# A transformer block with 32 experts on one core: the order of the source carried to both ends of the expert loop, and the softmax moved into the first expert

## The chip, the core and the metric
The kernel runs on one core of a Trainium2 chip. The core has a matrix engine (PE in the profile, with its weight loads as PEld), a vector engine (DVE), a scalar engine (ACT), a general one (POOL) and a queue engine (SP) that here only issues DMA. Each engine has its own row of instructions and works through it in order; semaphores tie the rows together. The metric is the device time of one execution in microseconds (us). The kernel before has a median of 1613.43 us over 3 runs (1612.79 to 1615.95).

## The reference
One decoder block over 512 tokens of 1024 channels: a convolution and an attention mixer first, then a mixture of experts, each behind a norm, and a final norm. The change touches only the second half:

```python
logits = hf @ w_router + b_router
top_v, top_e = lax.top_k(logits, 4)          # of 32 experts
gates = jax.nn.softmax(top_v, axis=-1)
...                                          # tokens gathered by expert
hc = xi @ w1[e] + b1[e]                      # 1024 -> 2 x 1024
g, u = hc[:, :1024], hc[:, 1024:]
hm = (u + 1) * (min(g, 7) * sigmoid(1.702 * g))      # u clipped to +-7
y  = hm @ w2[e] + b2[e]                      # 1024 -> 1024
...                                          # y weighted by its gate, added to its token
out = rms_norm(x + gate * moe, final_g)
```

## The kernel before
**Tokens and routing.** The 512 tokens are four blocks (b = 0 to 3) of 128 rows. For each block `logits` turns the normed tokens (`h2T`) and multiplies them by the router's weights into `pl`; `choose` finds the four largest logits and writes the 0/1 mask `Mb`; `places` counts, with matmuls into `prk`, at which row of its expert a token stands, and makes `hot`, the one-hot matrix by which the tokens of expert 0 are gathered (`x_mm`, matmuls into `px`; `x_out` copies them into `XT`, the instruction xT<-px). `norm_split` cuts the normed tokens into a high and a low part (`h2H`, `h2L`). After the last block the softmax of the four chosen logits follows: `nm`, four exponentials `g4` on ACT, one reciprocal, and for each block a product and a sum that spread the gates to the table `Gd` (128 tokens x 4 blocks x 32 experts).

**Ranking.** `rank_experts` sorts the experts by their count of tokens (`ms`, `pcf`, `pcp`, `kf`, `kp`, `rank`, `pmb`, `permi`): half of them are taken with up to 128 rows, the other half ("small") with up to 64, in turn. `order_places` and `order_gates` bring the tables of places and of gates into the order of the ranks by one transposition and one matmul each (`ptp`, `posT`, `pop`; `ptg`, `gT`, `pgo`, which gives `info`). From these tables `slot_hot`, `slot_mm` and `slot_out` (`pi`, `pis`, `si`) work out, for a pair of experts at a time, the token of each row (`dstx`) and its gate (`gat`).

**Experts.** The weights come in chunks of 1 MB (128x2048) through SP's DMA queue: 8 of w1 and 4 of w2 per expert. fp32 is done by splitting: ACT writes the high part `wh`, the DVE the rest `wl`; both have four buffers, and three splits are made ahead (`split_to`). A w1 chunk then costs 12 matmuls of 128x512 for a large expert (high with high, low with high, high with low). `steps` is the list of chunks, with those of w2 of an expert between those of w1 of the next. For a small expert `h_low` copies the lower half of the sums to `b1s` and `h_join` adds it by a shift matrix; `swiglu` forms `sg_s` and `sg_u`, `turn_h` transposes into `pz` and writes `hmh`; `finish` weights `y` and scatters it to the tokens.

**The end.** `bias_rows` prepares the rows of b2 times the gates (`b2s`, the tile w in the rows), `bias_part` multiplies them into eight PSUM areas of 128x512, two for each token block: those of block 1 and those of block 3 lie in one tile called ph, those of block 0 are called py and those of block 2 pz. The result of the last expert is not scattered but split (y, w<-y, w<-y,w) and added there by a one-hot matrix `place`. `joined` adds block b's sums to the tokens and squares them on ACT; `leave` takes the root (rs_v, rsx on ACT and DVE), scales and sends the block out.

**What sets the order.** A scheduler may move instructions of one engine, unless they are marked `keep_in_program_order`. The helpers MM, TR, ACT, TT, TS, STT and COPY mark what they issue while the flag `pinned` is up. It goes up ahead of the expert loop and down at the first chunk of expert 31. Reductions, maxima, reciprocals and copies that are issued directly are never marked.

## Time and profile before
| | |
|---|---|
| median of 3 runs | 1613.43 us |
| profiled execution, its span | 1611.79 us, 1610.0 us |
| PE busy | 1488.9 us, 92% of the span |
| DVE busy | 1349.4 us, 84% |
| ACT busy | 1043.4 us, 65% |
| chain that ended last, by engine | PE 55%, DVE 5%, ACT 4%, DMA 3%, issue 2% |
| splits | 352 on ACT (wh, 1913 ns each) and 352 on the DVE (wl, 2282 ns each) |

The times are those of one profiled execution, counted from its start. The front stages (convolution, attention) end at about 461 us, the experts fill the rest. Each row of a timeline is one group of instructions of one engine: start, length, engine, line, operation, output and input tile, shapes, count, and in brackets the idle time ahead of it with what ended it. Most lines read L55, since a helper issues them; go by the tiles.

### The profile page before, as it was taken

The numbers are of one execution on the slowest core, as the hardware profiler recorded it, in microseconds if no ns is written. First come the engines' busy times: TensorE is split into PE (matmuls) and PEld (weight loads), VectorE is DVE, ScalarE is ACT, GpSimd is POOL, SyncE is SP. The second block draws the span as 40 slices with busy tenths as digits, with TensorE's granted clock in tenths as the row PEclk, the third lists the DMA queues.
The fourth block names the chain that finished last, engine by engine and source line by source line (L and its number), as shares of the span: only waits on it lengthen the run. The fifth ranks groups of instructions, "written<-read, shape, count | busy, mean of one in ns | idle before, by whom it ended". The sixth has DMA issues, their size and how long they took to land.

```text
span 1610.0 us, 18694 instructions
## 1 busy us (share of the span) xinstructions
PE 1488.9 (92%) x6626; PEld 1126.6 (70%) x6626; DVE 1349.4 (84%) x1282; ACT 1043.4 (65%) x953; POOL 406.6 (25%) x200
## 2 busy tenths in 40 slices
PE   2998999999967999999999999999999999999975
PEld 2776667778755777777777777777777777777743
DVE  6799998743676798898988989989898898988874
ACT  3534764522354777777777777877777777777671
POOL 0323341300131032231322313223222232222630
PEclk9997999989988999999999999999999999999987
DMA  8623342343557799999999999999999999999963
GB/s 321 208 79 105 103 132 99 124 144 95 206 196 258 312 362 400 389 407 406 394 392 407 390 404 368 404 384 408 389 391 393 399 390 402 385 386 373 405 243 114
DMA packets 115647, 489.81 MB, mean 304 GB/s; under 512 B 12983, under 2 KB 35627, under 8 KB 80728
## 3 DMA queue, kind: packets, MB, share of 16 engines
q1 hardware_dynamic: 103088, 461.93, 72.9%
q0 software_dynamic: 9200, 24.21, 5.4%
q10 hardware_dynamic: 3256, 2.39, 0.5%
q8 instruction: 54, 0.88, 0.2%
q14 instruction: 49, 0.40, 0.1%
HBM read 477.66 MB, written 18.63 MB: 308 GB/s over the span
## 4 chain that ended last, share of the span: by engine, by line
PE 55%; DVE 5%; ACT 4%; DMA 3%; issue 2%; POOL 0%; DVEq 0%; ACTq 0%
PE ph L55 37%; PE py L55 14%; DVE wl L55 3%; DMA w<-in_w_exp_in_dram 3%; ACT wh L55 3%; PE pz L55 2%; PE px L55 1%; ACT b1s L55 1%; ACT sg_u L55 1%; PE pi L55 1%; DMA xg<-in_b_exp_out_dram 0%; DVE w L55 0%; DVE sg_u L55 0%; DVE x L55 0%; DVE b1s L55 0%
## 5 line engine op out<-in xcount | busy, mean ns | idle before, releaser
L55 DVE TENSOR_TENSOR wl<-w,wh 128x2048 fp32r<-128x2048 f32 x352 | 796.5, 2282 | 89.5 <-ACT wh L55 86.2
L55 ACT ACTIVATE wh<-w 128x2048 fp32r<-128x2048 f32 x352 | 664.6, 1913 | 139.1 <-DMA w<-in_w_exp_out_dram 44.6
L55 PE MATMUL ph<-wh,xT 128*128 128x512 f32 x1408 | 377.0, 405 | 2.0 <-ACT sg_u L55 2.0
L55 PEld LDWEIGHTS ph<-wh,xT 128*128 128x128 f32 x1408 | 261.2, 190 | 72.3 <-issue 12.6
L1280 POOL DMA_INDIRECT x1d<-y,dstx x31 | 182.2, 5879 | 333.4 <-DVE y L55 333.4
L55 PE MATMUL ph<-wl,xT 128*128 128x512 f32 x896 | 241.6, 392 | 0.0
L55 PEld LDWEIGHTS ph<-wl,xT 128*128 128x128 f32 x896 | 169.1, 189 | 36.5
L55 PE MATMUL py<-wh,hmh 128*128 128x512 f32 x496 | 144.1, 412 | 1.3 <-DVE hmh L55 1.3
L55 PE MATMUL py<-wl,hmh 128*128 128x512 f32 x496 | 133.2, 390 | 0.2 <-DVE wl L55 0.2
L55 DVE SCALAR_TENSOR_TENSOR cacc<-apad,cw,cacc 128x512 f32<-128x512 f32 x120 | 117.3, 990 | 1.2
L55 PE MATMUL ph<-w,xT 128*128 128x512 f32 x256 | 115.2, 593 | 0.0
L311 POOL TENSOR_TENSOR acc<-acc,adaw 128x1024 f32<-128x1024 f32 x28 | 72.7, 2600 | 162.1 <-ACT adaw L55 156.2
L55 PEld LDWEIGHTS py<-wh,hmh 128*128 128x128 f32 x496 | 89.7, 188 | 31.9 <-issue 12.7
L55 PEld LDWEIGHTS py<-wl,hmh 128*128 128x128 f32 x496 | 93.0, 188 | 20.5 <-DVE wl L55 0.7
L55 ACT ACTIVATE gh<-w 128x1024 fp32r<-128x1024 f32 (+1 forms) x48 | 43.8, 914 | 87.6 <-PE zg L55 35.1
L1190 POOL MEMSET xg<- 64x1024 f32 (+1 forms) x31 | 29.6, 958 | 275.3 <-PE px L55 275.3
L1191 POOL DMA_INDIRECT xg<-h2d,dstx x31 | 65.6, 2116 | 117.5 <-DVE gat L55 103.0
L55 DVE TENSOR_TENSOR gl<-w,gh 128x1024 fp32r<-128x1024 f32 (+1 forms) x48 | 60.3, 1257 | 37.5 <-ACT gh L55 37.2
L55 PEld LDWEIGHTS ph<-w,xT 128*128 128x128 f32 x256 | 46.3, 190 | 46.1 <-issue 45.9
L55 ACT ACTIVATE xT<-px 128x512 fp32r<-128x512 f32 x50 | 29.7, 595 | 61.4 <-PE px L55 57.7
L55 PE MATMUL py<-wh,hml 128*128 128x512 f32 x256 | 68.6, 390 | 0.0
L55 ACT ACTIVATE sg_s<-ph 128x1024 f32<-128x1024 f32 (+1 forms) x32 | 32.8, 1024 | 44.3 <-PE ph L55 43.9
(379 smaller groups left out, 2106.6 us busy)
## 6 DMA issues: line engine op xcount, KB each, us to landing
w<-in_w_exp_in_dram SPq DMA_DIRECT2D x256, 1024.0 KB, 9.7
w<-in_w_exp_out_dram SPq DMA_DIRECT2D x128, 1024.0 KB, 12.4
w<-in_w_in_dram SPq DMA_DIRECT2D x18, 1024.0 KB, 5.6
adaw<-in_w_ada_dram SPq DMA_DIRECT2D x16, 1024.0 KB, 7.4
w<-in_w_ada_dram SPq DMA_DIRECT2D x8, 1024.0 KB, 6.8
w<-in_w_out_dram SPq DMA_DIRECT2D x4, 1024.0 KB
x<-in_x_dram SPq DMA_DIRECT2D x4, 512.0 KB
w<-in_w_attn_out_dram SPq DMA_DIRECT2D x4, 512.0 KB, 3.4
```

The costliest lines, as they stand in the source:

```text
L55: ins = f(*args, **kw)
L311: nc.gpsimd.tensor_tensor(o, o, wi, op=OP.add)
L1190: nc.gpsimd.memset(xgs[p][:r], 0.0)
L1191: nc.gpsimd.indirect_dma_start(out=xgs[p][:r], out_offset=None, in_=h2d[:, :], in_offset=bass.IndirectOffsetOnAxis(ap=dstx[:r, p:p + 1], a ...
L1280: nc.gpsimd.indirect_dma_start(out=x1d[:, :], out_offset=bass.IndirectOffsetOnAxis(ap=dstx[:r, p:p + 1], axis=0), in_=y, in_offset=None, b ...
```

## The change
The flag becomes a set of engines. PE and DVE are marked from the last block's routing on, ACT from the expert loop on, and all three to the end, so that expert 31 and the final norm stand in the order of the source too. Reductions, maxima, reciprocals and copies are now marked with the rest. The softmax is done on the whole table in six operations within chunks 1 and 2 of expert 0: subtract the largest logit, one exponential (the only one on ACT), times `Mb`, sum, reciprocal, product. The slot matmuls of the first pair are done twice, once for the tokens (chunks 0 and 1) and once for the gates (chunks 4 and 5), the tables of the second pair two chunks later than before; for the first pass the gate columns of `info` are zeroed at the start. The ranking stands behind one split instead of three, the table of places behind three as before. In expert 31 `bias_rows` moves behind `h_low`.

```diff
+    pinned = set()
-            return tc.keep_in_program_order(ins) if pinned[0] else ins
+            return tc.keep_in_program_order(ins) if engine in pinned else ins
+    REDUCE = in_order(nc.vector.tensor_reduce, "DVE")      # also MAX, MAXI, RECIP
...
-        logits(NB - 1, 1)
-        for n in range(4):
+        pinned.update(("PE", "DVE"))
+        t = logits_t(NB - 1, 1)
+        for n in range(2):
             x_mm(n, range(NB - 1))
+        logits(NB - 1, 1, t)
         choose(NB - 1)
+        for n in range(2, 4):
+            x_mm(n, range(NB - 1))
         places(NB - 1)
...
-        TS(nm, v8[:, :, 0], -1.0, None, op0=OP.mult)
-        for b in range(NB):
-            ACT(g4[:, b, :], v8[:, b, :TOPK], AF.Exp, bias=nm[:, b:b + 1], accum_out=sm4[:, b:b + 1])
-        nc.vector.reciprocal(sm4, sm4)
-        TT(g4, g4, sm4[:, :, None].to_broadcast([P, NB, TOPK]), op=OP.mult)
-        for b in range(NB):
-            E2 = M.tile([P, TOPK, NE], F32, name="E2")
-            TT(E2, E4[:, b], g4[:, b, :, None].to_broadcast([P, TOPK, NE]), op=OP.mult)
-            nc.vector.tensor_reduce(Gd[:, b, :], E2.rearrange("p k e -> p e k"), axis=AX.X, op=OP.add)
...
+        def gates_exp():
+            TT(Gd, Gd, v8[:, :, 0:1].to_broadcast([P, NB, NE]), op=OP.subtract)
+            ACT(Gd, Gd, AF.Exp)
+        def gates():
+            sm4 = X.tile([P, NB], F32, name="sm4", bufs=1)
+            TT(Gd, Gd, Mb, op=OP.mult)
+            REDUCE(sm4, Gd, axis=AX.X, op=OP.add)
+            RECIP(sm4, sm4)
+            TT(Gd, Gd, sm4[:, :, None].to_broadcast([P, NB, NE]), op=OP.mult)
...
-        split_to(-1)
-        rank, pmb = rank_experts()
-        order_places(pmb)
+        split_to(-1, 1)
+        rank, pmb = rank_experts()
+        split_to(-1)
+        order_places(pmb)
...
-            if (kind, p, k) == ("w1", NE - 1, 0):
-                pinned[0] = False
...
                     if k == 0:
+                        slot_hot(0)
+                        slot_mm(0)
+                    if k == 1:
+                        slot_out(0, gate=False)
+                        gather(1)
+                        gates_exp()
+                    if k == 2:
+                        gates()
+                        biases(0)
+                    if k == 3:
                         order_gates(pmb)
+                        biases(1)
+                    if k == 4:
                         slot_mm(0)
...
-                    if k == 7:
                         b2s = raw_slot(F32R)
-                        bias_rows()
...
                         h_low(p)
+                        if p == NE - 1:
+                            bias_rows()
```

**Place 1: the DVE between the last block's mask and the first expert matmul.** `E`, `g` and `Gd` are the gates' spreading, `posb` and `hot` the places, `wl` a split. Before:

```order
L995 TENSOR_REDUCE Mb<-E_3195 128x32
L1062 RECIPROCAL sm_3633<-sm_3633 128x4
...
L1067 TENSOR_REDUCE Gd<-E_3651 128x32
L55 TENSOR_TENSOR wl<-w,wh 128x2048 x2
L55 SCALAR_TENSOR_TENSOR posb<-prk,Mb 128x32
L55 SCALAR_TENSOR_TENSOR posf<-prk,Mb 128x32
L55 TENSOR_TENSOR hot<-slots_92,posb 128x128
L55 TENSOR_TENSOR h2L<-h_3438,h2H 128x512 x2
L55 TENSOR_TENSOR wl<-w,wh 128x2048
L55 TENSOR_SCALAR shift<-jp 64x128
L1098 TENSOR_REDUCE ms<-Mb 128x32
```

and in the changed kernel:

```order
L55 TENSOR_REDUCE Mb<-E_3574 128x32
L55 SCALAR_TENSOR_TENSOR posb<-prk,Mb 128x32
L55 TENSOR_TENSOR hot<-slots_92,posb 128x128
L55 SCALAR_TENSOR_TENSOR posf<-prk,Mb 128x32
L55 TENSOR_TENSOR h2L<-h_3441,h2H 128x512 x2
L55 TENSOR_TENSOR wl<-w,wh 128x2048
L55 TENSOR_REDUCE ms<-Mb 128x32
...
L55 CAST sel<-pmb 64x32
L55 TENSOR_TENSOR wl<-w,wh 128x2048 x2
L55 TENSOR_TENSOR bdb<-blk,pmb 128x128
L55 CAST posT<-ptp 128x128
```

The gates' spreading is gone from this place, the places stand ahead of all splits, one split stands ahead of the ranking (`ms`), and two between the ranking and `posT`, which the first expert matmul follows.

**Place 1, ACT.** `g` are the exponentials of before, `xT` the gathered tokens of expert 0. Before:

```order
L55 ACTIVATE h2H<-h_3438 128x512 x2
L55 ACT_TABLE_LOAD
L55 ACTIVATE g_3634,sm_3633<-v_124,nm 128x4 x4
L55 ACTIVATE wh<-w 128x2048 x3
L55 ACTIVATE xT<-px 128x2x256 x4
L55 ACTIVATE b1s<-sg_u 64x1024
```

and now:

```order
L55 ACTIVATE h2H<-h_3441 128x512 x2
L55 ACTIVATE wh<-w 128x2048 x4
L55 ACTIVATE xT<-px 128x2x256 x4
L55 ACTIVATE wh<-w 128x2048
L55 ACT_TABLE_LOAD
L55 ACTIVATE Gd<-Gd 128x128
```

The table load and the exponentials have left the place ahead of the splits; four splits instead of three stand ahead of xT.

**Place 2: ACT in the last expert, behind the copies of its lower half.** `w<-xg` and `w<-pgt` are the bias rows, `sg_s` and `sg_u` the SwiGLU's halves. Before:

```order
L55 ACTIVATE b1s<-ph 64x1024 x2
L55 ACTIVATE wh<-w 128x2048
L55 ACTIVATE sg_s<-ph 64x1024
L55 ACTIVATE wh<-w 128x2048
L55 ACTIVATE w<-xg 64x1024
L55 ACTIVATE w<-pgt 32x512 x2
L55 ACTIVATE wh<-w 128x2048
L55 ACTIVATE sg_u<-ph 64x1024
```

and now:

```order
L55 ACTIVATE b1s<-ph 64x1024 x2
L55 ACTIVATE w<-xg 64x1024
L55 ACTIVATE w<-pgt 32x512 x2
L55 ACTIVATE wh<-w 128x2048
L55 ACTIVATE sg_s<-ph 64x1024
L55 ACTIVATE sg_u<-ph 64x1024
L55 ACTIVATE wh<-w 128x2048
```

Two splits have gone from between the copies and `sg_u` (they stand ahead of `b1s` now), and the two halves follow each other.

**Place 2, PE, from the last transposition to the end of w2.** `ph<-wh,hmh` and `ph<-wl,hmh` are the matmuls of w2 (one row of each is a chunk), the groups of `w` are bias rows. Before:

```order
L55 MATMUL pz<-ident,sg_u 128x64 x8
L55 MATMUL pz<-w 128x512
L55 MATMUL py<-w 128x512 x4
L55 MATMUL pz<-w 128x512
L55 MATMUL ph<-wh,hmh 128x512 x4
...
L55 MATMUL ph<-w 128x512 x4
L55 MATMUL pz<-w 128x512 x2
L55 MATMUL ph<-wh,hmh 128x512 x4
```

and now:

```order
L55 MATMUL pz<-ident,sg_u 128x64 x8
L55 MATMUL ph<-wh,hmh 128x512 x4
...
L55 MATMUL py<-w 128x512 x4
L55 MATMUL ph<-w 128x512 x4
L55 MATMUL pz<-w 128x512 x4
L55 MATMUL ph<-wh,hmh 128x512 x4
```

All twelve bias matmuls stand between the second and the third chunk; six of them stood ahead of the first.

**Place 3: the DVE from the last expert's result to the first two blocks' scaling.** `x_11636` is block 0, `x_11638` block 1, `x_11640` block 2, `x_11642` block 3. Before:

```order
L55 SCALAR_TENSOR_TENSOR y<-ph,gat,g2b 128x512 x2
L55 TENSOR_TENSOR w<-y,w 128x512 x2
L55 TENSOR_TENSOR x_11636<-py,x_11636 128x512 x2
L55 TENSOR_TENSOR x_11640<-pz,x_11640 128x512 x2
L55 TENSOR_SCALAR rs_v<-ssq 128x1
L55 TENSOR_TENSOR x_11638<-ph,x_11638 128x512 x2
L153 RECIPROCAL rsx<-rsx 128x1
L55 TENSOR_TENSOR x_11642<-ph,x_11642 128x512
...
L55 SCALAR_TENSOR_TENSOR w<-x_11636,rsx,w 128x1024
```

and now:

```order
L55 SCALAR_TENSOR_TENSOR y<-ph,gat,g2b 128x512
L55 TENSOR_TENSOR w<-y,w 128x512
L55 SCALAR_TENSOR_TENSOR y<-ph,gat,g2b 128x512
L55 TENSOR_TENSOR w<-y,w 128x512
L55 TENSOR_TENSOR x_11636<-py,x_11636 128x512 x2
L55 TENSOR_TENSOR x_11638<-ph,x_11638 128x512 x2
L55 TENSOR_SCALAR rs_v<-ssq 128x1
L158 RECIPROCAL rsx<-rsx 128x1
...
L55 SCALAR_TENSOR_TENSOR w<-x_11636,rsx,w 128x1024
L55 TENSOR_TENSOR x_11640<-pz,x_11640 128x512 x2
```

Before, all four blocks are joined before the first is scaled, block 2 ahead of block 1; now each block's joining and the scaling of the block before it alternate, on ACT (Square, root) as on the DVE.

## Rows read from the trace of the kernel before

**Rows 1.** Windows: stretch, length, busy time and count per engine, PE clock, DMA.

```profile
553.20:620.07 66.87, 65.86 (x289) 49.49 (x288) 60.47 (x39) 51.01 (x36) 16.44 (x7) 1.00 0.97 381
...
1558.90:1569.10 10.20, 0.01 (x1) 0.02 (x1) 10.11 (x8) 9.63 (x9) 0.00 (x0) 0.57 0.00 0
```

**Rows 2.** Timeline of the DVE, last routing to first expert matmul.

```profile
467.26 0.18 DVE L1062 RECIPROCAL sm<-sm 128x4 f32<-128x4 f32 x1 [3.97 <-ACT g L55]
...
469.63 4.48 DVE L55 TENSOR_TENSOR wl<-w,wh 128x2048 fp32r<-128x2048 f32 x2
...
479.51 1.56 DVE L55 TENSOR_SCALAR kf<-kf,kp 128x32 f32<-128x32 f32 x1
...
482.24 0.29 DVE L1125 CAST posT<-ptp 128x128 bf16<-128x128 f32 x1 [0.23 <-PE ptp L55]
```

**Rows 3.** Timeline of ACT in the same stretch.

```profile
464.70 1.28 ACT L55 ACT_TABLE_LOAD   x1
...
467.13 5.49 ACT L55 ACTIVATE wh<-w 128x2048 fp32r<-128x2048 f32 x3
476.07 1.19 ACT L55 ACTIVATE xT<-px 128x512 fp32r<-128x512 f32 x2 [3.45 <-issue]
```

**Rows 4.** Timeline of PE, from the last gathering through expert 0.

```profile
474.69 0.87 PE L55 MATMUL px<-hot,h2H 128*128 128x128 f32 x3 [9.31 <-DVE hot L55]
...
482.63 3.25 PE L55 MATMUL ph<-wh,xT 128*128 128x512 f32 x8
...
492.20 0.80 PE L55 MATMUL pgo<-bdf,gT 128*128 128x128 f32 x2 [5.29 <-DVE bdf L55]
...
496.76 0.63 PE L55 MATMUL pi<-hot,info 128*8 128x256 f32 x4
```

**Rows 5.** Groups of PE in expert 31's first half: count, busy us, mean ns.

```profile
L55 PE MATMUL pgt<-ident,Gd 128*32 128x128 f32 x4 | 0.8, 272 | 0.0
```

**Rows 6.** Timeline of all engines, last w1 chunk to w2 of expert 31.

```profile
1549.43 1.07 PE L55 MATMUL ph<-wh,xT 128*128 128x512 f32 x4
1550.34 1.07 PE L55 MATMUL ph<-wl,xT 128*128 128x512 f32 x4
...
1551.44 1.93 ACT L55 ACTIVATE b1s<-ph 64x1024 fp32r<-64x1024 f32 x2 [7.14 <-PE ph L55]
...
1558.51 1.06 ACT L55 ACTIVATE w<-xg 64x1024 fp32r<-64x1024 f32 x1
...
1559.47 1.16 ACT L55 ACTIVATE w<-pgt 32x512 fp32r<-32x512 f32 x2
...
1562.48 1.00 ACT L55 ACTIVATE sg_u<-ph 64x1024 f32<-64x1024 f32 x1
...
1567.82 1.21 DVE L55 SCALAR_TENSOR_TENSOR sg_u<-sg_s,sg_u 64x1024 f32<-64x1024 f32 x1
...
1573.58 2.08 PE L55 MATMUL ph<-wh,hmh 128*128 128x512 f32 x4
...
1580.91 0.92 PE L55 MATMUL pz<-w 64*128 64x512 f32 x2
```

**Rows 7.** Timeline of all engines from the last w2 matmul on.

```profile
1585.72 1.41 DVE L55 SCALAR_TENSOR_TENSOR y<-ph,gat,g2b 128x512 f32<-128x512 f32 x2 [12.70 <-PE ph L55]
...
1587.23 1.29 DVE L55 TENSOR_TENSOR w<-y,w 128x512 fp32r<-128x512 f32 x2
...
1590.21 3.10 PE L55 MATMUL ph<-w 64*128 64x512 f32 x8
...
1593.35 1.29 DVE L55 TENSOR_TENSOR x<-ph,x 128x512 f32<-128x512 f32 x2 [1.22 <-PE ph L55]
...
1594.67 1.06 ACT L55 ACTIVATE w<-x 128x1024 f32<-128x1024 f32 x1 [1.45 <-DVE x L55]
...
1600.63 0.16 DVE L153 RECIPROCAL rsx<-rsx 128x1 f32<-128x1 f32 x1
...
1601.41 1.28 DVE L55 SCALAR_TENSOR_TENSOR w<-x,rsx,w 128x1024 f32<-128x1024 f32 x1
```

More of the change, by code (lines that the diff above doesn't have):

```diff
@@ L49, in hybrid_block, with in_order @@
     nc = tc.nc
-    pinned = [False]
-    def in_order(f):
+    pinned = set()
+    def in_order(f, engine):
         def g(*args, **kw):
             ins = f(*args, **kw)
-            return tc.keep_in_program_order(ins) if pinned[0] else ins
+            return tc.keep_in_program_order(ins) if engine in pinned else ins
         return g
-    MM = in_order(nc.tensor.matmul)
-    TR = in_order(nc.tensor.transpose)
-    ACT = in_order(nc.scalar.activation)
-    TT = in_order(nc.vector.tensor_tensor)
-    TS = in_order(nc.vector.tensor_scalar)
-    STT = in_order(nc.vector.scalar_tensor_tensor)
-    COPY = in_order(nc.vector.tensor_copy)
+    MM = in_order(nc.tensor.matmul, "PE")
+    TR = in_order(nc.tensor.transpose, "PE")
+    ACT = in_order(nc.scalar.activation, "ACT")
+    TT = in_order(nc.vector.tensor_tensor, "DVE")
+    TS = in_order(nc.vector.tensor_scalar, "DVE")
+    STT = in_order(nc.vector.scalar_tensor_tensor, "DVE")
+    COPY = in_order(nc.vector.tensor_copy, "DVE")
+    REDUCE = in_order(nc.vector.tensor_reduce, "DVE")
+    MAX = in_order(nc.vector.max, "DVE")
+    MAXI = in_order(nc.vector.max_index, "DVE")
+    RECIP = in_order(nc.vector.reciprocal, "DVE")
     x2d = x[0]
@@ L967, in hybrid_block, with logits_t @@
         pls = {}
-        def logits(b, hf):
-            if hf == 0:
-                pls[b] = bank("pl")
+        def logits_t(b, hf):
             ps = bank("ph")
@@ L978, in logits @@
             ACT(t, ps, AF.Copy)
+            return t
+        def logits(b, hf, t=None):
+            if hf == 0:
+                pls[b] = bank("pl")
+            t = t or logits_t(b, hf)
             for k in range(4):
@@ L1108, in rank_experts @@
             rank = X.tile([P, 1], F32, name="rank", bufs=1)
[L1109 removed]
+            REDUCE(rank, kf, axis=AX.X, op=OP.add)
             pmb = X.tile([P, NE], BF, name="pmb", bufs=1)
@@ L1166, in slot_mm, with slot_out @@
             COPY(pis[j], ps[:8, :2 * P])
-        def slot_out(j):
+        def slot_out(j, to=True, gate=True):
             ps = bank("pi")
@@ L1174, in slot_out @@
             es = slice(2 * j, 2 * j + 2)
-            STT(dstx[:, es], si[:, 0:13:12], FAR, si[:, 1:14:12], op0=OP.add, op1=OP.add)
+            if to:
+                STT(dstx[:, es], si[:, 0:13:12], FAR, si[:, 1:14:12], op0=OP.add, op1=OP.add)
             if j == NE // 2 - 1:
                 STT(tokf, si[:, 12:13], FAR, si[:, 13:14], op0=OP.add, op1=OP.add)
-            TT(gat[:, es], si[:, 2:15:12], si[:, 3:16:12], op=OP.add)
+            if gate:
+                TT(gat[:, es], si[:, 2:15:12], si[:, 3:16:12], op=OP.add)
         g2b = X.tile([P, D], F32, name="g2b", bufs=1)
@@ L1297, in hybrid_block, with split_to @@
         made = []
-        def split_to(i):
-            while todo and sum(j > i for j in made) < AHEAD:
+        def split_to(i, ahead=AHEAD):
+            while todo and sum(j > i for j in made) < ahead:
                 j, key = todo.pop(0)
@@ L1438, in hybrid_block, with biases @@
                 nc.gpsimd.dma_start(b1r[j][32 * i:32 * i + 32], b1[:, j * FE:(j + 1) * FE])
-        for j in range(2):
+        def biases(j):
             js = slice(j * FE, (j + 1) * FE)
```

65 lines of the change are left out of this document (28 added, 37 removed).

## The prediction

> **What bounds the kernel now.** I read the table of stretches first. In the steady experts TensorE is busy 65.86 of 66.87 us at the full clock [rows 1], so every microsecond won or lost before them or after them is carried to the end, and nothing inside them can be won by moving work. The change leaves the order of experts 1 to 30 as it was, row for row on every engine; only the two ends are reordered. At the rear TensorE stands almost still for 10.20 us [rows 1], then follow the last four chunks of w2, and from the last matmul (1593.35) to 1602.69 it is the DVE's turn [rows 7]; the output DMA closes the span 7.3 us later. The chain of waits runs through these ends by PE, DVE and ACT in turn, so I read the timelines there, engine by engine.
>
> **The head, before the first matmul of expert 0.** On the DVE the reciprocal of the softmax waits 3.97 us for the four exponentials; eight operations spread the gates, then come two splits of 2.24 us each from 469.63 on [rows 2], and only then the one-hot of the last block's places, for which TensorE waits 9.31 us, until 474.69 [rows 4]. The first expert matmul starts at 482.63 [rows 4]. ACT loads a table (1.28 us) and does the exponentials before its first split at 467.13 [rows 3].
> In the new order the DVE goes from the logits straight to the places. The one-hot's users then start about 9 us earlier (474.69 less two splits, 4.48, less the gates and the wait, some 4.5), near 465.7, and the gather matmuls behind it, which end before 479 now, end before 470. That is not the new start of expert 0. ACT does four splits ahead of the four copies xT: from 464.7, four times 1.83 (5.49 for three [rows 3]) ends at 472.0, and the first copy (1.19 for two) at 472.6 to 473. The ranking's second matmul (pcp) waits for ACT, since its PSUM bank is one that xT empties. So the chain from kf starts near 473.3 instead of 479.51; from kf to posT it takes 2.73 us now, 0.23 of them idle; two small copies, some 0.3, are added, then two splits, 4.48, stand ahead of posT with bdb, 0.2, and from posT to the first matmul it is 0.39 [rows 2, 4]: 473.3 + 2.5 + 0.3 + 4.5 + 0.2 + 0.4 = 481.2. Gain at this point 1.4, not 9.
> **Inside expert 0** the gates are now made. Before, TensorE waits 5.29 us at the product pgo that turns the gates [rows 4]. After: chunk 0 takes some 4.1 us (3.25 for its first eight matmuls, nearly twice the later pitch [rows 4], and four more behind), three warm chunks 2.72 each (0.91 for four [rows 6]), slot matmuls 0.9, so chunk 3 ends at 494.4. On the other side: the fifth split waits for chunk 0 to free its buffers (485.3), 1.9 on ACT, 2.28 on the DVE, then subtract and Exp about 1.0 (no row has them; an estimate from posT's 0.29 for the same 128x128, twice that at most for two operands), one more split pair 1.9 + 2.3, four small operations 1.3: the gates stand at 495.8 and TensorE has waited 1.4. The copy gT stands behind a bias subtraction of 1.2 and a split of 2.28 in the DVE's row: with bdf 0.3 and gT 0.3 another 3.9. Together 5.3 against 5.29. The slot matmuls of pair 0 are done twice: 0.63 [rows 4] and 0.3 for the transposition. So 0.9 to 1.0 of the 1.4 is given back, and the head is worth -0.4. Bounds: -6 us if the gate waits vanish, +1.5 if the start does not move.
> A rule weighed here: the row shows the table load at 464.70, 1.28 us, with the first exponential 0.01 us behind it [rows 3]. The Trainium skill ("ScalarE: Activation LUTs", "What ACT_TABLE_LOAD costs") puts a switch at about 1.28 plus a drain of 1.38. By that, taking the load out of the way would start the splits 1.4 us sooner than I reckon, and the head would gain 1.4; the trace shows no such drain, so I leave it at the row. The new load stands in expert 0 where ACT waits for buffers anyway.
>
> **Expert 31, first half.** Four transpositions of the gates (0.8 in all [rows 5]) leave the full stretch of TensorE for a place behind its last w1 chunk, where it waits anyway: -0.8.
>
> **Expert 31, from its hidden rows to w2.** Now the bias rows stand right behind the two copies b1s. ACT after b1s (ends 1553.4 [rows 6]): wait for the product on the DVE, queued behind a split (to 1554.9), w<-xg 1.06, w<-pgt 1.16, one split 1.91, then both SwiGLU copies of 1.0 each [rows 6], end 1561.1. The DVE's split ends at 1561.4, its two SwiGLU operations 0.7 and 1.2: 1563.3, where it was 1569.03 [rows 6]: -5.7. Behind it stand the same three operations as before (split, y of expert 30, hmh), so the first w2 matmul moves from 1573.58 to 1567.9. But all twelve bias matmuls (0.43 each: 0.92 for two [rows 6]) now stand between chunk 1 and chunk 2; before, six of them filled the wait. Six more cost 2.6. So w2 ends 3.1 earlier; bounds 1.5 (five more matmuls at twice the pitch and the bias product late) and 5.
>
> **The end**, counted from the last w2 matmul, T, which releases y (1585.72 [rows 7]). Before, the last scaling ends at 1602.69, T + 17.0. In the new order every step is queued:
> y and its two halves alternate between DVE and ACT instead of going in pairs: the second low half at T + 4.25 (was 1588.52, T + 2.8 [rows 7]). Sixteen more place and bias matmuls: eight at 0.23 and the last eight 3.10 [rows 7], end T + 9.4 (was 7.65). Block 1's sum waits for all of them, as it does now (1593.35, idle until the last matmul), because its two banks lie in one tile with block 3's; but now block 0's scaling stands behind it. From T + 9.4: pair 1.29, Square 1.06 with 0.18 to read it out, the root of block 0 which ACT has queued behind that Square 0.2, reciprocal to scaling 0.78, scaling 1.28, and 0.1 of hand-overs: 4.85, all in series, because block b+1 is joined ahead of block b's leaving. Three such rounds end at T + 23.95, the last block's root, reciprocal and scaling take 2.45 more: T + 26.4. Loss 9.4. Lower bound 6.6, if block 1 could start when its own banks are written (T + 6.6); upper 10.5. The 7.3 us of output DMA behind the last scaling stay; the last transfer is no longer crowded by others, which may give back up to 0.5.
>
> **Sum.** -0.4 - 0.8 - 3.1 + 9.4 = +5.1 on the profiled execution's 1611.79 us (span 1610.0 and 1.79 around it): 1616.9. That execution lies 1.64 below the median of the runs, so on their scale 1613.43 + 5.1 = **1618.5 us**.
>
> **Rivals.**
> (1) Forecast, slower: 1614.5 to 1621.5.
> (2) The gates come in time: the place is expert 0's chunk 3; the price is the 5.3 us of ptg and pgo. It decides when the last gate product on the DVE ends before chunk 3 does and gT isn't queued behind a split. For it: softmax is off the head, and TensorE's slow first chunk gives the DVE time. Against: two split pairs stand in the same queues. Then +5.1 - 5.3 = -0.2: 1613.2, not slower.
> (3) The end is less serial: block 1 needn't wait for block 3's matmuls (-2.8) and the last DMA lands 0.5 sooner: 1615.2, within the noise. Against it: the idle before x<-ph at 1593.35.
> (4) Both, or the start of expert 0 comes 3 us sooner because the ranking doesn't wait for xT: 1609 to 1611, faster. Against it: the wait on ACT is there in the program.
> (5) w2 starts colder. The clock over the 10.20 us wait is 0.57 on the mean, and the first four w2 matmuls still take 2.08, though bias matmuls ran ahead of them; now nothing does. Eight more at twice the pitch add 1.8, and the later waits of expert 0 (psh) may cost 1 more: 1621.1.
> The Trainium skill ("TensorE: Matmul & The Clock Gate", "What's actually happening") says the array's default is the throttled clock and that activity releases it. By that rule the bias matmuls before w2 did useful warming, and losing them is case 5; the row neither confirms it nor denies it.
>
> **Chances.** (1) 0.54, (2) 0.15, (3) 0.12, (4) 0.08, (5) 0.11. A change under 0.2% (3.2 us) can't be told from none here. Slower: (1) nearly all and (5), with a little taken off for cases between: 0.64. Same: (2), (3) and that little: 0.25. Faster: (4) and the lower edge of (2): 0.11. The range of the forecast alone is 1614.5 to 1621.5; to leave no more than 2 in 10 out it reaches down to (2): 1611.5 to 1621.5.
>
> **What would show it.** In the new profile: the DVE's one-hot of the last block near 465 and the first expert matmul near 481 (479 or less: the ranking didn't wait for xT). TensorE idle about 5 us around ptg and pgo. SwiGLU of expert 31 done 5 to 6 us earlier relative to its last w1 chunk, w2 only 3 to 4. From the last w2 matmul to the last scaling 26 us, with ACT's roots each behind the next block's Square and the outputs leaving one by one every 4.8 us. If that stretch takes 20 or less, or if the idle in expert 0 is under 2 us, I am wrong.

## The result and the profile after

The changed kernel takes 1625.76 us (median of 4 runs, 1623.14 to 1630.71) against 1614.17 us for the kernel before in runs beside it (4 runs, 1612.79 to 1615.95): ratio 1.008, 95% interval 1.0058 to 1.0102. It is slower, as forecast, but by 11.6 us and not by 5.1; 1625.76 lies above the range given (1611.5 to 1621.5). The span of the profiled execution went from 1610.0 to 1623.5 us, that is +13.5.

The account below cuts both traces at the same instructions. "px" is the first matmul into the tile px, which gathers the tokens of expert 0, "S0" to "S31" the starts of the SwiGLU products (the DVE's SCALAR_TENSOR_TENSOR on sg_u), one for each expert, and T the start of y in expert 31, as in the prediction. "Half clock" means the lower of TensorE's two levels, 1.2 GHz (0.50 in the rows), "full clock" the upper, 2.4 GHz.

| stretch | before | after | difference | forecast |
|---|---|---|---|---|
| start to px | 458.32 | 459.92 | +1.6 | 0 |
| px to S0 (routing, expert 0) | 65.00 | 66.46 | +1.5 | -0.4 |
| S0 to S28 (steady) | 934.01 | 936.30 | +2.3 | 0 |
| S28 to the last w1 matmul | 94.08 | 93.56 | -0.5 | -0.8 |
| last w1 matmul to the end of S31 | 17.62 | 12.01 | -5.6 | -5.7 |
| to the first w2 matmul of expert 31 | 4.55 | 4.05 | -0.5 | 0 |
| first w2 matmul to T | 12.14 | 16.60 | +4.5 | +2.6 |
| T to the end of the last scaling | 16.97 | 27.44 | +10.5 | +9.4 |
| sum | | | +13.7 | +5.1 |

The start of px varied from 455.89 to 462.20 over the profiles of all kernels here, and a second profile of the unchanged kernel before has it at 459.85 (458.32 in the first), so +1.6 is chance. The output behind the last scaling takes 0.1 less, which leaves the +13.5 of the span. The other lines are the matter of the experiments.

The windows of after (stretch, length, busy time and count by engine, PE clock, DMA), answering to [rows 1]:

```profile
460.50:471.25 10.75, 10.75 (x54) 10.75 (x53) 3.53 (x13) 6.75 (x7) 4.04 (x4) 0.51 0.78 293
485.40:491.60 6.20, 6.20 (x18) 4.59 (x19) 3.94 (x4) 2.38 (x2) 0.00 (x0) 0.52 0.99 367
556.00:622.50 66.50, 65.59 (x287) 49.09 (x286) 60.52 (x39) 50.61 (x36) 16.46 (x7) 1.00 0.97 379
```

Look at the clock in the first row: TensorE is busy without a break and still runs at 0.51, its lower level. It gathers the tokens of expert 0 there, mostly in 128x128 matmuls. The third row looks like its counterpart of before; the loss of the steady experts is too small to be seen in it.

The DVE of after in the head (start, duration, engine, line, operation, out<-in, count, idle before and what ended it), answering to [rows 2]:

```profile
471.62 0.19 DVE L55 SCALAR_TENSOR_TENSOR posb<-prk,Mb 128x32 bf16<-128x32 f32 x1 [3.80 <-PE prk L55]
471.85 0.29 DVE L55 TENSOR_TENSOR hot<-slots,posb 128x128 fp32r<-128x128 bf16 x1
...
476.96 2.47 DVE L55 TENSOR_SCALAR kf<-kf,kp 128x32 f32<-128x32 f32 x1
...
480.48 4.47 DVE L55 TENSOR_TENSOR wl<-w,wh 128x2048 fp32r<-128x2048 f32 x2
...
485.02 0.27 DVE L55 CAST posT<-ptp 128x128 bf16<-128x128 f32 x1
```

The one-hot hot of the last block, forecast near 465.7, came at 471.85: prk stands in TensorE's written order behind the gathering matmuls that run at half clock, and the DVE waits 3.80 for it.

TensorE of after in the same place, answering to [rows 4]:

```profile
485.35 0.29 PE L55 MATMUL pop<-bdb,posT 128*128 128x128 bf16 x1 [4.45 <-DVE posT L55]
485.40 3.76 PE L55 MATMUL ph<-wh,xT 128*128 128x512 f32 x8
488.96 1.91 PE L55 MATMUL ph<-wl,xT 128*128 128x512 f32 x4
...
500.77 0.33 PE L55 MATMUL ptg<-ident,Gd 128*128 128x128 f32 x1 [0.53 <-DVE Gd L55]
504.74 0.55 PE L55 MATMUL pgo<-bdf,gT 128*128 128x128 f32 x2 [3.64 <-DVE gT L55]
```

The first expert matmul starts 25.48 us after px, where it was 24.31; the two splits of 4.47 are in the wait of 4.45 ahead of it. The waits for the gates, ptg and pgo, are 0.53 and 3.64, together 4.17 (forecast 5.3).

The rear of after, all engines, answering to [rows 5, 6]:

```profile
1556.08 0.60 PE L55 MATMUL pgt<-ident,Gd 128*32 128x128 f32 x4
...
1556.28 1.94 ACT L55 ACTIVATE b1s<-ph 64x1024 fp32r<-64x1024 f32 x2 [0.81 <-PE ph L55]
...
1564.88 1.00 ACT L55 ACTIVATE sg_u<-ph 64x1024 f32<-64x1024 f32 x1
...
1567.03 1.22 DVE L55 SCALAR_TENSOR_TENSOR sg_u<-sg_s,sg_u 64x1024 f32<-64x1024 f32 x1
...
1572.30 2.08 PE L55 MATMUL ph<-wh,hmh 128*128 128x512 f32 x4 [2.82 <-DVE hmh L55]
...
1578.26 1.77 PE L55 MATMUL py<-w 64*128 64x512 f32 x4
...
1583.36 1.84 PE L55 MATMUL ph<-wh,hmh 128*128 128x512 f32 x4
...
1585.00 1.91 PE L55 MATMUL ph<-wl,hmh 128*128 128x512 f32 x4
```

SwiGLU comes as early as forecast. The twelve bias matmuls (1578.26 to 1583.4, 0.43 each) stand ahead of chunk 2, and the eight matmuls behind them take 1.84 and 1.91 for four, at a granted clock of 0.54 (1583.36 to 1586.70), where a run of four takes 1.07 at the full clock [rows 6]. Counted from start to start, the +4.5 is 2.55 for the six more bias matmuls, which the forecast had, and 1.9 for slower chunks, which it had not; 1.4 of that is chunk 2.

The end of after, all engines, answering to [rows 7]:

```profile
1588.90 0.75 DVE L55 SCALAR_TENSOR_TENSOR y<-ph,gat,g2b 128x512 f32<-128x512 f32 x1 [14.46 <-PE ph L55]
...
1596.79 3.31 PE L55 MATMUL ph<-w 64*128 64x512 f32 x8
...
1600.14 1.29 DVE L55 TENSOR_TENSOR x<-ph,x 128x512 f32<-128x512 f32 x2 [5.11 <-PE ph L55]
...
1602.52 0.19 ACT L55 ACTIVATE rsx<-rs_v 128x1 f32<-128x1 f32 x1
...
1603.51 1.28 DVE L55 SCALAR_TENSOR_TENSOR w<-x,rsx,w 128x1024 f32<-128x1024 f32 x1
...
1608.09 1.28 DVE L55 SCALAR_TENSOR_TENSOR w<-x,rsx,w 128x1024 f32<-128x1024 f32 x1
...
1612.66 1.28 DVE L55 SCALAR_TENSOR_TENSOR w<-x,rsx,w 128x1024 f32<-128x1024 f32 x1
...
1615.06 1.28 DVE L55 SCALAR_TENSOR_TENSOR w<-x,rsx,w 128x1024 f32<-128x1024 f32 x1
```

The first three scalings leave 4.58 us apart, the last 2.40 later, and the DVE stands idle 5.11 us before block 1 is joined: the picture of the prediction, with a later start (T + 11.2 instead of T + 9.4) and a little shorter rounds (4.58, not 4.85). The later start comes from the eight matmuls that stand ahead of the last eight: they take 3.25 us (1593.54 to 1596.79) at a granted clock of 0.55, where the forecast had eight at 0.23. The last eight take 3.31, much as before (3.10 [rows 7]).

### The profile page after: what moved, and what is told of

Same layout as the page of the kernel before. It is cut to its first block, busy times and chain, and to the rows that moved or that the text cites. A ratio compares the mean times of both kernels' runs of the same rounds, so it can differ in the third digit from the quotient of the medians.

```text
span 1623.5 us, 18704 instructions
## 1 busy us (share of the span) xinstructions
PE 1499.6 (92%) x6632; PEld 1132.7 (70%) x6632; DVE 1350.8 (83%) x1282; ACT 1042.4 (64%) x946; POOL 375.8 (23%) x200
## 4 chain that ended last, share of the span: by engine, by line
PE 70%; DVE 14%; ACT 7%; DMA 4%; issue 3%; POOL 1%; SPq 0%; ACTq 0%; DVEq 0%; POOLq 0%
PE ph L55 40%; PE py L55 15%; DVE cacc L55 5%; ACT wh L55 3%; PE zg L55 3%; PE pb L55 2%; PE px L55 2%; PE po L55 2%; DVE wl L55 2%; PE pz L55 2%; DVE gl L55 2%; DMA adaw<-in_w_ada_dram 2%; DMA w<-in_w_exp_in_dram 1%; ACT b1s L55 1%; ACT sg_u L55 1%
## 5 line engine op out<-in xcount | busy, mean ns | idle before, releaser
L1292 POOL DMA_INDIRECT x1d<-y,dstx x31 | 150.6, 4857 | 360.9 <-DVE y L55 360.9
L1203 POOL DMA_INDIRECT xg<-h2d,dstx x31 | 62.1, 2004 | 109.0 <-DVE gat L55 93.8
```

The costliest lines, as they stand in the source:

```text
L1203: nc.gpsimd.indirect_dma_start(out=xgs[p][:r], out_offset=None, in_=h2d[:, :], in_offset=bass.IndirectOffsetOnAxis(ap=dstx[:r, p:p + 1], a ...
L1292: nc.gpsimd.indirect_dma_start(out=x1d[:, :], out_offset=bass.IndirectOffsetOnAxis(ap=dstx[:r, p:p + 1], axis=0), in_=y, in_offset=None, b ...
```

## The experiments

Every ratio is against the kernel before, in runs beside it on the same chip, with its 95% interval.

**The kernel before once more** (no edit).

> The kernel before, unchanged, profiled a second time. Two pieces of the 13.5 us by which the changed kernel's profiled span is longer have no instruction to answer for them: 1.6 us that it is late already at 455 us, where both programs are the same, and 2.3 us that build up evenly over experts 1 to 29 (SwiGLU of expert 1 3.0 us late, of expert 29 5.35), where the order is the same. Theory A, these are differences between executions or chips: this profile differs from the first one of the same kernel by 1 us or more at 455 us, or in the time from expert 1 to expert 29, or both. Theory B, they belong to the change: this profile repeats the first one within 0.4 us in both stretches.

Measured: 1613.87 us, span 1612.1. Cut at the same instructions it gives 65.44 from px to S0, 900.41 from S1 to S28 (900.36 in the first profile of before, 902.70 in after), 17.62, 4.56, 12.18 and 16.97 behind it. The start of px is 1.5 later than in the first profile. So theory A holds for the start, which is chance, and theory B for the steady stretch: differences of 0.1 in the rear and of some tenths in the steady stretch carry meaning, and the head can differ by half a microsecond. In this profile TensorE's clock fell to 0.50 near 460 already, as in after, and the head took only 0.44 longer: in the old order the one-hot comes 15.93 us after px at either clock, because the softmax and two splits hold it, not TensorE.

**The old order of the rear alone.**

```
 for i, (kind, p, k) in enumerate(steps):
+    if (kind, p, k) == ("w1", NE - 1, 0): pinned.clear()
...  (bias_rows and place where they stood before)
```

> The changed kernel with the tail of the kernel before: marks dropped at expert 31's first chunk, bias rows before its lower-half copies. What is left is the head. Theory A (the head costs about 1.2 us, from its clock and the extra slot work, and the 3.9 us without an instruction are chance): 0 to +2.5 us against the kernel before, ratio 1.000 to 1.0015. Theory B (the 3.9 us belong to the change): +4 to +5.5, ratio 1.0025 to 1.0035. My prediction's head (-0.4): ratio 0.9995. By all of them the stretch from the last w2 matmul to the last scaling is back at 17 us.

Measured: 1616.82 us, ratio 1.0015 (1.0002 to 1.0027). Behind the last w1 matmul the stretches are 17.62, 4.56, 12.35 and 16.97, those of before. What is left is in front of expert 31: 66.48 from px to S0 and 936.30 from there to S28, 1.5 and 2.3 more than in before. The trace thus keeps both losses, as theory B has it; the times give 2.4 us, the upper edge of theory A, with an interval (0.3 to 4.4) that reaches into theory B.

**The end alone set free.**

```
+pinned.clear()
 yhl = weighted(NE - 1)
```

> The changed kernel with the marks dropped only behind the last w2 chunk, so that the scheduler orders the final norm as before. Theory (the end's alternation of joining and scaling is most of the loss): last w2 matmul to last scaling 17 us instead of 27.4, the time 9 to 11 us below the changed kernel's, ratio to the kernel before 1.000 to 1.0025. Rival (the end is limited by what the place matmuls and the outputs allow, not by the order): less than 4 us come back, ratio over 1.005.

Measured: 1612.3 us, ratio 0.999 (0.9971 to 1.0009); T to the last scaling 17.00. The same stretch of the trace:

```profile
1591.88 1.29 DVE L55 TENSOR_TENSOR x<-py,x 128x512 f32<-128x512 f32 x2 [0.92 <-PE py L55]
...
1600.72 2.48 DVE L55 SCALAR_TENSOR_TENSOR w<-x,rsx,w 128x1024 f32<-128x1024 f32 x2
...
1603.88 1.28 DVE L55 SCALAR_TENSOR_TENSOR w<-x,rsx,w 128x1024 f32<-128x1024 f32 x1
```

Joins go ahead as banks come, and the small steps of one block's root run under the join of the next; two scalings then stand back to back. The written end is worth 10.4 us in the trace, nearly the whole loss. Some 3.6 of it come before block 1 is joined (T + 7.7 here, T + 11.2 in after), the rest from the rounds. By the ratios (1.0080 and 0.9990) it would be 14 us; the twelve runs spread from 1606.51 to 1619.78, and the profiled one is in their middle.

**A written order with all joins ahead of all scalings.**

```
-joined(0)
-for b in range(NB):
-    if b + 1 < NB: joined(b + 1)
-    leave(b)
+for b in (0, 2, 1, 3): joined(b)
+for b in (0, 2, 1, 3): leave(b)
```

> The changed kernel, all marks kept, with the source of the end written in another order: blocks 0, 2, 1, 3 are joined, then the four are scaled in that order. It tells whether the price is the source's order or being in a fixed order at all. If it is the alternation: y and its halves still cost 1.45 us, the joins end at T + 14, the roots wait for nothing but the Squares, four scalings of 1.3 with their chains of 0.8 behind; last scaling near T + 21 to 22 instead of 27.4, time 5 to 6.5 us below the changed kernel's. If any fixed order costs the same: within 2 us of the changed kernel's.

Measured: 1620.59 us, ratio 1.005 (1.0035 to 1.0065); T to the last scaling 24.28, 3.2 better than after and 2 to 3 worse than expected. Two of the DVE's last scalings:

```profile
1603.36 1.28 DVE L55 SCALAR_TENSOR_TENSOR w<-x,rsx,w 128x1024 f32<-128x1024 f32 x1
...
1605.75 1.28 DVE L55 SCALAR_TENSOR_TENSOR w<-x,rsx,w 128x1024 f32<-128x1024 f32 x1
```

They stand 2.4 us apart: scaling, rs_v, a root on ACT, four small operations, next scaling. Block 1 is joined at T + 11.2 here, as in after, so this order saved only in the rounds. A better order in blocks is not enough; what the free end has besides is that the small steps of several blocks are interleaved (argued from its rows: no run wrote such an order by hand).

**Where the steady loss comes from: 64 bytes.** The order of experts 1 to 30 is the same in both kernels, yet they take 2.3 us longer. A difference is that the new tile sm4, which takes 32 bytes as placed, pushes the experts' tiles hmh, hml and y on by 32 bytes in SBUF, the on-chip memory of the tiles. That they stood at a multiple of 512 bytes before is my reckoning of the allocation; no trace shows addresses.

```
-sm4 = X.tile([P, NB], F32, name="sm4", bufs=1)
+sm4 = X.tile([P, 16], F32, name="sm4", bufs=1)[:, :NB]
```

> The changed kernel with the small softmax tile sm4 allocated 64 bytes long instead of 16 (32 as placed), so that the tiles behind it in SBUF, hmh and hml above all, stand on an address that 64 divides, as in the kernel before; no instruction changes. Theory (the placement slows every w2 matmul: pitch 0.233 us against 0.2265 in the stretches of py): from the SwiGLU of expert 1 to that of expert 28 it takes 900.4 us as in the kernel before, not 902.7 to 903.2, and the time falls by 2.3 us (0.14%). Rival (the marks or the softmax slow the steady experts in another way): 902.7 again, time unchanged.

Measured: 1627.14 us, ratio 1.0082 (1.0053 to 1.0111); S1 to S28 903.80: not restored. The theory in this form, 64 bytes, fell.

**The kernel before with 32 bytes more.**

```
+gap = X.tile([P, NB], F32, name="gap", bufs=1)
+nc.vector.memset(gap, 0.0)
```

> The kernel before with an unused tile of 32 placed bytes ahead of ssq (one clearing instruction of a few elements), which moves hmh and hml by 32 bytes and nothing of the order. Theory of the placement: expert 1 to expert 28 takes 902.7 instead of 900.4, +2.3 us, ratio 1.0014. Rival (it is the change's order): 900.4 and ratio 1.000.

Measured: 1618.06 us, ratio 1.0031 (1.0018 to 1.0045); S1 to S28 903.23, against 900.36. Shifting tiles alone brings the steady loss, with nothing else of the change. The ratio stands for 5 us, more than the 2.9 in the trace and above the 1.0014 expected; where the other 2 us lie stays open, since the run that was profiled (1614.72) is one of the two shortest of the ten. Together with the run before it: the place matters, and 64 bytes are not the grain.

**128, 256 and 512 bytes** for sm4 in the changed kernel, the edit as above with 32, 64 and 128 columns.

> The changed kernel with the small tile sm4 widened from 32 to 128 bytes, which puts hmh, hml and y of the experts at a multiple of 128 bytes (they stood at a multiple of 512 before the change, at 32 bytes past one after it, and at 64 past one in the 64-byte run). Placement theory with 128 bytes as the grain: the stretch from the second to the 29th SwiGLU goes back from 902.7 to about 900.4 us. Placement theory with a larger grain: it stays at 902.7 to 903.8. Rival (not the place of these tiles, but something else that the change brings into the steady experts): stays at 902.7.

> The same with 256 bytes: hmh, hml and y stand 256 bytes past a multiple of 512. Grain of 128 or 256 bytes: the stretch of 27 experts takes about 900.4 us. Grain of 512 bytes, or the rival: 902.7 to 903.8.

> The same with 512 bytes: hmh, hml and y stand at a multiple of 512 again, as before the change. Placement theory at any grain: 900.4 us for the stretch of 27 experts, and a median about 2.3 us under the changed kernel's 1625.8, near 1623. Rival: 902.7 and no gain.

Measured, S1 to S28: 903.99 with 128 bytes, 900.71 with 256, 901.90 with 512. The first two were run once, 1628.85 and 1627.99 us; the last six times, 1622.32 us, ratio 1.0057 (1.0042 to 1.0073), beside 1.0080 of after, so that the intervals overlap and only the trace shows the gain. Two groups of TensorE's matmuls of w2, one that loads hmh and one that loads hml (us 600 to 1450; duration ns min/median/max), in before and in after, then the first group in e6, e9 and e10:

```profile
L55 PE MATMUL py<-wl,hmh x408: 388/389/398, 602.8 to 1447.6; 128*128 128x512 f32 x136
L55 PE MATMUL py<-wh,hml x208: 388/389/395, 601.9 to 1423.9; 128*128 128x512 f32 x104
```

```profile
L55 PE MATMUL py<-wl,hmh x404: 395/396/401, 605.9 to 1444.4; 128*128 128x512 f32 x135
L55 PE MATMUL py<-wh,hml x208: 395/396/396, 604.9 to 1429.2; 128*128 128x512 f32 x104
```

```profile
L55 PE MATMUL py<-wl,hmh x406: 387/395/401, 602.8 to 1449.9; 128*128 128x512 f32 x136
```

```profile
L55 PE MATMUL py<-wl,hmh x404: 388/395/404, 604.9 to 1444.5; 128*128 128x512 f32 x135
```

```profile
L55 PE MATMUL py<-wl,hmh x404: 387/389/398, 607.6 to 1444.2; 128*128 128x512 f32 x135
```

The median of the first group goes 389, 396, 395, 395, 389: a shift of 256 bytes restores it, 128 does not. These matmuls follow each other every 227.6 ns in before, every 233.4 in after and every 227.9 at 256 bytes (mean over some 303 pairs); those that load hml every 227.9, 233.6 and 228.1, and the third group, wh with hmh, every 230.7, 232.7 and 232.1, so that 256 bytes restore little of it. The matmuls of w1, which load xT, are hardly slower (228.3 and 228.4 for wh). Added up from start to start between S1 and S28, the three groups of w2 take 3.2 us more in after than in before and TensorE's other matmuls 0.4 more, while its waits are 1.3 shorter: together the loss of 2.3. Whether it is the place of hmh or that of hml was not tried apart. The 512-byte run has the pitch of 227.9 too; its 1.2 us more than at 256 bytes are one wait in one expert:

```profile
861.19 0.73 PE L55 MATMUL py<-b1s,shift 64*128 64x512 f32 x2 [2.18 <-ACT b1s L55]
```

In the other twelve waits of this kind it is 0.98.

The rear came out longer than in after in the four runs with a wider sm4, though its order is the same: 17.4 to 20.1 us from w2 to T (16.60 in after) and 28.2 to 29.9 from T to the last scaling (27.44). The granted clock fell at other places there: in the 256-byte run the last eight bias matmuls take 5.26 us at 0.50, in after 3.31 at 0.92. That, with a later px (461.04) and a longer head (67.52), is why the 256-byte run is no faster as a whole. What decides where the clock falls, and whether the wider tile has a part in it, was not found.

**The written order only from the experts on** (routing and gathering left to the scheduler, softmax in expert 0).

```
-pinned.update(("PE", "DVE"))
...
-pinned.add("ACT")
+pinned.update(("PE", "DVE", "ACT"))
 for i, (kind, p, k) in enumerate(steps):
```

> The changed kernel with the marks set only at the expert loop, as before; the softmax stays in expert 0. The scheduler then puts one split instead of three between the last block's logits and the table of places. What is told apart: whether the fixed order of the last routing or the softmax inside expert 0 costs the head its time. If the fixed order: first expert matmul 3 to 4.5 us earlier after the first gathering matmul than the changed kernel's 25.5, end of expert 0 (first SwiGLU) 1.5 to 4 us earlier than its 66.5 (kernel before 65.0). If the waits inside expert 0 take it all back (splits late there): first matmul earlier, but the SwiGLU within 0.7 of 66.5. PE's clock during the gathering matmuls: at half as in the changed kernel, since PE's row there is nearly the same.

Measured: 1627.67 us, ratio 1.0092 (1.0068 to 1.0115); px to S0 68.26, longer than either expectation had it. The first expert matmul comes 25.29 us after px (25.48 in after), and the gathering ran at the full clock, not at half as expected. The written order of the routing is no loss against the scheduler's; with the scheduler the one-hot comes 16.11 us after px, and the rest is no shorter.

**Six of the twelve bias matmuls back in the wait** before w2 of expert 31.

```
 if (p, k) == (NE - 2, 3):
     turn_h(NE - 1)
...
+    for n in (0, 1, 4):
+        bias_part(n)
...
-    for n in range(6):
+    for n in (2, 3, 5):
         bias_part(n)
```

> The changed kernel with six of the twelve bias matmuls put back ahead of expert 31's first w2 chunk, into the wait for hmh. From the first w2 matmul to the last it took 12.15 us in the kernel before and 16.5 in the changed one. Theory (twelve slow matmuls in the middle cost their own 2.6 us and let the clock fall for the last two chunks, another 1.8): 12.2 us, -4.3 in time. Rival (the clock falls for another reason): 13.9, -2.6. First w2 matmul no later than 0.5 us.

Measured: 1623.4 us (5 runs, 1615.61 to 1624.33), ratio 1.0057 (1.004 to 1.0074); w2 to T 12.08, as expected, and chunk 2 runs at the full clock again (1.20 and 1.07 for four), but the first w2 matmul came 7.83 us after SwiGLU instead of 4.05, where no more than 0.5 was expected. Its rear, all engines:

```profile
1561.42 1.27 DVE L55 SCALAR_TENSOR_TENSOR y<-py,gat,g2b 128x1024 f32<-128x1024 f32 x1
...
1562.84 2.92 PE L55 MATMUL py<-w 64*128 64x512 f32 x4 [2.31 <-DVE y L55]
...
1565.69 1.51 PE L55 MATMUL pz<-w 64*128 64x512 f32 x2
...
1567.13 2.08 PE L55 MATMUL ph<-wh,hmh 128*128 128x512 f32 x4
```

The banks py that the bias matmuls fill belong to expert 30 until the DVE has read them for y (1562.69), and by then hmh is due. So they stand in no wait: the six take 4.3 us (1562.84 to 1567.13) and push w2 back by 3.8, and the two stretches together win 0.7. The forecast's idea that six of them could be hidden there holds for the old order only, where SwiGLU is later.

The profiled execution is the shortest of the five, and its head shows why:

```profile
457.00:463.00 6.00, 6.00 (x58) 6.00 (x58) 4.55 (x14) 2.00 (x5) 3.40 (x3) 1.00 0.51 206
```

The gathering matmuls run at the full clock here (58 in 6 us; in after 54 in 10.75), the one-hot comes 6.83 us after px instead of 11.93, and px to S0 takes 60.83 instead of 66.46. Of the twelve profiles with the new order of the routing, nine have the half clock there (66.4 to 67.5 us to S0 where nothing else was changed in the head) and three the full one. What decides it was not found: in the 4 us ahead of px TensorE was busy for 2.94 us in after and for 2.97 here, both at 1.00. Only the profiled run of a kernel shows its head, and the other four runs of this one took 1623.3 to 1624.33 us, so part of the spread between runs of one kernel may be this.

**order_places and the rank's comparison.** The splits that stand ahead of posT moved behind it, and the TENSOR_SCALAR of 2.47 us replaced.

```
-split_to(-1)
 order_places(pmb)
+split_to(-1)
...
-TS(kf, kf, kp[:, 0:1], None, op0=OP.is_gt)
+TT(kf, kf, kp[:, 0:1].to_broadcast([P, NE]), op=OP.is_gt)
```

> The changed kernel with order_places ahead of the two splits that stood before it in the source's order (wl x2, 4.47 us on VectorE between sel and bdb/posT), and the comparison for the rank as a tensor_tensor instead of the tensor_scalar that took 2.47 us and ended with GpSimd's clearing of xg. Theory (in the head the written order lets the first expert matmul wait for 4.5 us of splits and 2.2 us of that comparison): the first expert matmul starts 6 to 7 us earlier after the first gathering matmul (25.5 down to about 19), first SwiGLU 66.5 down to 60 to 62, median about 1620. Rival (TensorE's chunks after it are bound by the splits or by the gates anyway): the first matmul comes earlier but the first SwiGLU stays within 1 us of 66.5.

Measured: 1629.49 us, ratio 1.0092 (1.0072 to 1.0112). The first expert matmul came 20.97 us after px (25.48 in after), and yet S0 at 70.27 instead of 66.46. TensorE:

```profile
481.06 3.75 PE L55 MATMUL ph<-wh,xT 128*128 128x512 f32 x8
...
489.80 1.02 PE L55 MATMUL pi<-hot,info 128*8 128x256 f32 x4 [4.07 <-DVE hot L55]
490.62 3.62 PE L55 MATMUL ph<-wh,xT 128*128 128x512 f32 x8
```

The wait was not taken away but cut off chunk 0 and put behind it: pi needs hot, which the DVE makes behind the same splits. And a chunk that follows such a wait runs at the half clock here (0.50; 3.62 to 3.76 for eight, against 1.99 for the second chunk of after), so two waits make two slow chunks. Neither expectation was met: the theory fell, and the rival, right in its direction, had S0 within 1 us of 66.46. The DVE did kf in 0.19 here, but the next TENSOR_SCALAR took 2.02 (see the last section).

**Both losses out: the end free and 256 bytes** (the edits of e3 and e10 together), **and the same with hot ahead of the splits too.**

```
 order_places(pmb)
+slot_hot(0)
 split_to(-1)
```

> The changed kernel with both losses that the runs have shown taken out: the order of the end left to the scheduler (as in the run with the free end) and the three tiles of the experts at a multiple of 256 bytes. If the account is complete, what is left are the gains of expert 31 (5.6 us in its first half, less 4.4 for the bias matmuls, 0.5 each for the transposes and the first matmul of w2) against about 1 us in the head: 27 experts in 900.5, last scaling 17.0 after the last w2 matmul, and 1 to 5 us under before, ratio 0.9965 to 0.9995, about 1609.5. Rival (something else in the changed order costs as well): no faster than before, ratio 1.0 or more.

> The same, with the head in another order besides: order_places and the first slot_hot ahead of the two splits, and the rank's comparison as a tensor_tensor. Theory (in the run with the places first the 4.4 us were lost again because the slot matmuls waited 4.07 us for hot, which stood behind two splits): with hot ahead of them too, the first slot matmul follows chunk 0 at once, and the first SwiGLU comes 3 to 5 us earlier than in the run beside it, ratio about 0.995. Rival (the head is bound by what comes later, the splits and the gates, and by the half clock): the first SwiGLU within 1.5 us of the run beside it and no measurable gain over it.

Measured: 1610.14 us, ratio 0.9981 (0.9966 to 0.9995), and 1607.9 us, ratio 0.9971 (0.9957 to 0.9986). Both beat the kernel before, by 3.1 and 4.7 us as the ratios have it. With the two losses out, the changed kernel's gains in expert 31 are real: 12.06, 4.05 and T + 17.0 in both traces, S1 to S28 901.78 (with one wait of 1.06 that the other profile does not have) and 900.55. But w2 to T takes 17.55 and 16.11 (12.14 in before), so that of the stretch from S28 to T only 1.6 and 3.0 us are won. The rest of the gain in these two profiles is the head: from px to S0 they take 62.64 and 62.24, both with the full clock in the gathering, as by chance in e8. The two can't be told apart. In the second the slot matmuls follow chunk 0 at once, as the theory said, but then:

```profile
485.25 0.29 PE L55 MATMUL pi<-ident,pis 8*128 8x8 f32 x2 [1.31 <-DVE pis L55]
...
493.46 0.47 PE L55 MATMUL ptg<-ident,Gd 128*128 128x128 f32 x1 [2.25 <-DVE Gd L55]
497.44 0.80 PE L55 MATMUL pgo<-bdf,gT 128*128 128x128 f32 x2 [3.50 <-DVE gT L55]
```

TensorE waits 7.06 us for what the DVE does between its splits: what was won in front (the first expert matmul at px + 16.45 instead of 20.57) is waited for at the gates. The rival stands: the head is bound by the DVE's and ACT's splits and by the gates, and in both runs by a held copy of 2.25 us on the DVE besides (last section).

## Why the prediction was wrong

The direction and the mechanism of the largest term were right; the sum was too small by 8.6 us on the trace's scale (13.7 against 5.1); 1.6 of that is the chance start of px, the rest lies in five terms.

- **The end, +9.4, measured +10.5.** The serial rounds are as described (block b+1 joined ahead of block b's leaving, the root behind the next Square), and e3 and e4 show it. Mis-sized: the sixteen last matmuls, reckoned to end at T + 9.4 (the terms written there make 9.2), end at T + 11.2, since eight of them took 3.25 at a clock of 0.55 and not 1.84, while a round takes 4.58 and not 4.85. Rival 3 (less serial) fell.
- **w2 of expert 31, -3.1, measured -1.6** (-5.6 - 0.5 + 4.5). The SwiGLU part was right to 0.1. Failed: "Six more cost 2.6". Six more cost 2.55 by themselves, but the chunk behind them runs at a clock of 0.54 (3.75 for eight instead of 2.1), and the slower chunks cost 1.9 more: that is rival 5's price of 1.8, though most of it falls behind the bias matmuls and not ahead of them. e8 shows both: with six fewer in the middle w2 takes 12.08, and what they do in the wait does not make the first four w2 matmuls any faster (2.08 in after and in e8). The rule of the Trainium skill weighed there ("TensorE: Matmul & The Clock Gate", "What's actually happening"), that activity releases the clock, is therefore not shown at this place by these six; the gathering at 0.51 with TensorE busy for all of 10.75 us goes against it as it was read here.
- **The steady experts, 0, measured +2.3.** Failed: "nothing inside them can be won by moving work", taken as nothing can be lost. The rows were the same and their order too; the tiles were not in the same place. e6 (loss without the change) and e10 (change without the loss) show it in the stretch from S1 to S28. I had not compared where the tiles lie.
- **The head, -0.4, measured +1.5.** Failed: "near 465.7" for the one-hot. I took the gathering matmuls at the full clock of before's trace; the new order puts the routing behind them, and at half clock they end 5 us later. At full clock the head wins 2.4 to 4.2 (62.64 and 60.83 against 65.00), which lies within the bounds of -6 and +1.5 but isn't the forecast either. Inside expert 0 the gate waits were 4.17 instead of 5.3, and chunk 0 took 5.3 and not 4.1. The table load that left the head says nothing new on a drain behind it: in after it stands at 491.12, 1.28 us, with 2.81 us idle before Exp, which waits for the DVE. No run here shows the drain of which the Trainium skill tells ("ScalarE: Activation LUTs", "What ACT_TABLE_LOAD costs"); in before the first exponential stands 0.01 behind the load.
- **The transposes, -0.8, measured -0.5.** Right but for 0.3.

All five terms erred to the same side (the last by 0.3 only), and three of them (bias matmuls, end, head) for one reason: a duration of before was taken at the clock that it had there. The term with the value 0, for 27 experts and 900 us, had no bound at all.

## What to carry to other kernels

A written order must be as fine as the waits it runs through: at the end of a kernel, where every step waits for another engine, blocks written one after the other cost 10.4 us here against an order that interleaves the small steps. A wait that is moved rather than removed can cost more than before: in e12 each of the two waits was followed by a chunk at half clock (3.62 and 3.75 us for eight matmuls instead of 2.0). When a change adds or removes even a small tile, compare where the tiles of the hot loop lie, and shift them back (by a multiple of 256 bytes here) before judging the order. And a kernel whose head runs at either clock by chance needs more than one profile before a gain of 2 us there is believed.

## What the runs showed of the hardware that was not expected

- Moving the tiles hmh, hml and y by 32, 64 or 128 bytes lengthened the pitch of two groups of matmuls, which load hmh and hml, from some 228 ns to 233, and the steady stretch by 2.3 to 3.6 us over 27 experts (after, e5, e6, e9); a move by 256 or 512 bytes left the pitch at 228 (e10, e11).
- TensorE's granted clock fell to 0.50 within 1.2 us of px and stayed there through 128x128 matmuls that kept the engine busy without a break (10.75 of 10.75 us at 0.51 in after), in nine of twelve profiles, and held 1.00 through the same matmuls in three.
- A TENSOR_SCALAR on the DVE was held until GpSimd (POOL) had cleared xg. In after the one of 2.47 us, shown with the head above, ends at 479.43, and this clearing at 479.38:

```profile
477.52 1.86 POOL L1202 MEMSET xg<- 64x1024 f32 x2
```

In e12 the comparison for the rank is a TENSOR_TENSOR and is done before the clearing starts, so it shows nothing; the TENSOR_SCALAR behind it (0.24 in after) is held instead. In e14, as in e13, the clearing comes earlier and holds a CAST that takes 0.23 in after, and TensorE's pcf waits 3.58 for it. In this order:

```profile
477.62 2.02 DVE L55 TENSOR_SCALAR pmb<-rankp,rank 128x32 bf16<-128x32 f32 x1
477.75 1.86 POOL L1202 MEMSET xg<- 64x1024 f32 x2
```

```profile
470.54 2.25 DVE L55 CAST mb<-ms 128x128 bf16<-128x128 f32 x1
470.84 1.86 POOL L1202 MEMSET xg<- 64x1024 f32 x2
```

That other operations pass during the clearing is seen in before, where two SCALAR_TENSOR_TENSOR take 0.18 and 0.15 in it and the TENSOR_SCALAR behind them 1.56 [rows 2]:

```profile
479.16 1.86 POOL L1190 MEMSET xg<- 64x1024 f32 x2
479.22 0.18 DVE L55 SCALAR_TENSOR_TENSOR kf<-pcf,keyf 128x32 f32<-128x32 f32 x1
```

In after, e12 and e14 the held operation starts before the clearing does (by 0.56, 0.13 and 0.30), at the time of a DMA issue of GpSimd; what holds it then is not shown.
